# The last stage of a hybrid attention layer in another order: block 2's operands beside block 3's out product, then MLP 2, gates 0 and 2, MLP 3, gate 3

## The chip, the cores and the metric

The kernel runs on one core of one Trainium2 chip. The metric is the device time of one execution in microseconds (us). The kernel before takes 3191.57 us (median of 3 runs, 3189.75 to 3192.46). The core's engines run beside each other: TensorE (PE, matmuls), VectorE (DVE), ScalarE (ACT), GpSimd (POOL) and SyncE (SP, which issues all the transfers named here). [...] Each engine takes its instructions in the order of the program, so an instruction that waits holds up all that stand behind it on its engine; SyncE's transfers are issued in that order too.

## The reference, cut to what matters

One layer with a model width of 1024 over 2048 prompt tokens and 32 sample tokens. Both attentions come first; what follows them, for each token, is:

```python
x = x + concat(attn_a, attn_b) @ w_out              # out product, residual
c = rmsnorm(x, g_mlp)
x = x + relu(c @ w_up) ** 2 @ w_down                # MLP, 1024 -> 4096 -> 1024
x = x + sigmoid(x @ w_ple_gate) * (p @ w_ple_proj)  # gate; p has 256 columns
y = rmsnorm(x, g_final)                             # final rows
```

Everything is float32. Tokens do not meet in these five lines, so blocks of tokens may be done in any order; within a block the lines must follow one another.

## The kernel before, in words

The tokens form four blocks: 0, 1 and 2 of 512, and 3 of 544 with the sample tokens. Activations lie transposed, with the width on the partitions (8 tiles of 128) and the tokens on the free axis. A float32 product is made of three passes: each operand is split into a high part (ScalarE rounds it) and a low part (GpSimd or VectorE subtracts the high one), and `mm3` issues high x high, high x low and low x high (lines 215, 216, 217). Weights are split in the same way, in halves called pieces, as they come in (`wr` is the raw weight; lines 175 and 180 are the splits' instructions on GpSimd and ScalarE, 165 and 186 are those of the GpSimd and VectorE subtraction elsewhere).

`outproj(b)` makes the residual of a block in 8 steps of d: a weight, a load of x (`hd`), 8 x 3 matmuls into `ops`, an addition on VectorE (line 935), the square for the norm, and a store into the scratch tensor `hS` in HBM. `oload(b)` loads the attention's output of a block (`oraw`), normalizes half of it (line 910) and splits it into `oact`. `colnorm(b)` makes from the squares the reciprocal norm `r` (lines 1017 to 1020 on VectorE are its last steps).

Blocks 0 and 1 go through their MLP (`mlp`) with plain products. Blocks 2 and 3 use `mlp7`, in which each up product of a 2 x 2 partition is made of seven products of half the width. Its operands are seven sums of the normalized rows, each split in two, made by `cparts(b)` in four quarters k: two loads of rows from `hS` into `tmp`, two scalings by gain and norm (line 976), five VectorE splits and two GpSimd splits (line 165) and four VectorE sums (lines 988 to 991); ScalarE makes the seven high parts. The results lie in `cs` (14 tiles for one block). In `mlp7`, up products go to `ups`, VectorE forms their combinations (line 1135), ScalarE squares (lines 1139, 1140), and the down products `dps` are added to `h` by VectorE (line 1124). It makes its own sums of the weights on VectorE (lines 1163 to 1166).

`gate(b)` splits the 8 tiles of h into `hu` (or into the tiles of `cs` for block 3), loads the split p (`pT`) and makes, for each of 8 d, a gate product `gps` and a projection `pps`, a sigmoid on ScalarE and VectorE, and an addition to h. `hu` and `pT` together take all 20 tiles of the ring `u` in the pool `uh`. `final(b)` transposes h by TensorE (`yp`), takes the squares (`junk`), scales and stores y.

`weave(main, side, step)` runs two generators in turn: after every step-th yield of `main` one step of `side`, and the rest of `side` at the end. The order of the program on each engine follows from the order of these calls. All loads and stores of this part are issued by SyncE (line 156). Tiles come from pools with rings; a new tile waits for the last reader of the one whose place it takes. Pools on the left are a stack, so that what is opened after another was closed lies on its place.

The last stage, in `run`, starts when MLP 1 and gate 1 are done:

1. out product 2, with the loads of block 3's attention output (`oload(3)`, into the pool `acth`);
2. out product 3; behind its first step the norm `r2`; behind its end `acth` is closed and `cs` opened on its place. The pool `hh`, with two buffers for h, lies elsewhere and has been open from the start, so that h of block 0 can be loaded early;
3. gate 0, with the norm `r3` behind its first step and `cparts(2)` beside it;
4. MLP 2, with `final(0)` beside it; h of block 2 is loaded ahead of it;
5. gate 2, with `cparts(3)` beside it;
6. MLP 3, with `final(2)` beside it; h of block 3 is loaded ahead of it;
7. gate 3 and `final(3)` together.

Of the kernel before, what the change touches and what calls it, by code (L numbers as in the profile page):

```python
# [12 lines left out]
F32 = mybir.dt.float32  # L13
# [6 lines left out]
P = 128  # L20
D = 1024
# [12 lines left out]
BLK = 544  # L34
# [48 lines left out]
def drain(gen):  # L83
    for _ in gen:
        pass
# [57 lines left out]
class Kern:  # L143
# [1115 lines left out]
                        self.pool_tt(hv, hv, sg, ALU.add)  # L1259
                yield  # L1260

    def final(self, b, h, up, fk, mm, md=None):
        nc, a = self.nc, self.a
        t0 = 512 * b
        sts, yns = {}, {}
        phased = md is not None

        def side(c0, tn, q):
            if phased:
                sts[c0] = st_all[:, c0 // P]  # L1270
            elif q == 0:
                sts[c0] = fk.tile([P, 2], F32, tag="fst", bufs=6, name="fst")
            st = sts[c0]
            yp = (md if phased and q == 1 else mm).tile([P, 512], F32, tag="mm", name="yp")
            for k in range(4):
                nc.tensor.transpose(yp[:tn, P * k : P * k + P], h[:, 4 * q + k, c0 : c0 + tn], self.ident)
            if phased and q == 1:
                yns[c0, q] = yp
            else:
                yns[c0, q] = up.tile([P, BLK], F32, tag="u", name="yn")[:, :512]  # L1280
                if phased:
                    nc.vector.tensor_tensor(yns[c0, q][:tn], yp[:tn], self.gf[:tn, :512], op=ALU.mult)
                else:
                    nc.vector.tensor_copy(yns[c0, q][:tn], yp[:tn])
            junk = up.tile([P, BLK], F32, tag="u", name="junk")[:tn, :512]
            nc.scalar.activation(junk, yp[:tn], AF.Square, accum_out=st[:tn, q : q + 1])

        if phased:
            st_all = fk.tile([P, 5, 2], F32, tag="fsa", name="fsa")
            nc.gpsimd.memset(st_all, 1.0)  # L1290
            for c0, tn in toks(b):
                side(c0, tn, 0)
                yield
        def emit(c0, tn, r):
            tt = t0 + c0
            dst = a["y_prompt"][0, tt : tt + tn] if tt < SP else a["y_sample"][0, tt - SP : tt - SP + tn]
            for q in range(2):
                src = yn = yns[c0, q]
                if phased and q == 1:
                    yn = up.tile([P, BLK], F32, tag="u", name="yo")[:, :512]  # L1300
                g = self.gf[:tn, 512 * q : 512 * q + 512]
                if phased and q == 0:
                    nc.scalar.activation(yn[:tn], src[:tn], AF.Copy, scale=r)
                else:
                    nc.vector.scalar_tensor_tensor(yn[:tn], src[:tn], r, g, op0=ALU.mult, op1=ALU.mult)
                self.dma(dst[:, 512 * q : 512 * q + 512], yn[:tn])

        if phased:
            for c0, tn in toks(b):
                side(c0, tn, 1)  # L1310
            ss = fk.tile([P, 5], F32, tag="fss", name="fss")
            nc.vector.tensor_tensor(ss, st_all[:, :, 0], st_all[:, :, 1], op=ALU.add)
            r = self.rsqrt(fk, ss, 5, 1.0 / D, EPS, nc.vector, "rfa")
            for i, (c0, tn) in enumerate(toks(b)):
                emit(c0, tn, r[:tn, i : i + 1])
            return
        for c0, tn in toks(b):
            side(c0, tn, 0)
            side(c0, tn, 1)
            st = sts[c0]  # L1320
            nc.vector.tensor_tensor(st[:tn, 0:1], st[:tn, 0:1], st[:tn, 1:2], op=ALU.add)
            emit(c0, tn, self.rsqrt(fk, st[:tn, 0:1], 1, 1.0 / D, EPS, nc.vector, "rf", tn, 5))
            yield

    def run(self):
        tc, nc, a = self.tc, self.nc, self.a
        with ExitStack() as top:
# [13 lines left out]
            mm = opened(top, "mm", MM, PSUM)  # L1341
# [94 lines left out]
            wk = opened(sq_, "wk", 1)  # L1436
# [49 lines left out]
            self.nt = 8  # L1486
            self.rawp = Rings((self.wp, "wr"), (wk, "wr"))
            self.gfin(fk)
            hh = opened(top, "hh", 2, side="right")
            with ExitStack() as x:  # L1490
                act = Sized(opened(x, "acth", 2), BLK, True)
                weave(self.outproj(2, wk, oa[2], md, acc[2]), self.oload(3, wk, act, oa), 1, 0, OW)
                g = self.outproj(3, wk, oa[3], md, acc[3])
                next(g)
                r2 = self.colnorm(acc[2][0], 2, 1.0 / D, wk, mm, "mm", None)
                drain(g)
            cs = Sized(opened(top, "cs", 14), None)
            ops = {}
            h = hload(hh, BLK, 0)
            g = self.gate(0, h, up, None, md, wk)  # L1500
            next(g)
            r3 = self.colnorm(acc[3][0], 3, 1.0 / D, wk, mm, "mm", None)
            weave(g, self.cparts(2, wk, cs, ops, r2), 1)
            f = self.final(0, h, up, fk, mm)
            h = hload(hh, BLK, 2)
            m = self.mlp7(2, h, ops[2], wk, up, mm, md)
            for _ in range(2):
                next(m)
            weave(m, f, 1)
            g = self.gate(2, h, up, None, md, wk)  # L1510
            next(g)
            weave(g, self.cparts(3, wk, cs, ops, r3), 1)
            f = self.final(2, h, up, fk, mm)
            h = hload(hh, BLK, 3)
            m = self.mlp7(3, h, ops[3], wk, up, mm, md)
            for _ in range(2):
# [53 lines left out]
```

## Time and profile before

| what | value |
|---|---|
| median of the runs | 3191.57 us (3189.75 to 3192.46, 3 runs) |
| the profiled execution's own time | 3197.78 us |
| its span, first to last instruction | 3196.0 us |
| mean granted clock of TensorE in it | 0.977 of full speed |
| out product 3 | 2213.7 to 2272.4 us of the span |
| gate 0 | 2272.4 to 2329.0 us |
| MLP 2 | 2329.0 to 2671 us |
| gate 2 | 2671 to 2743 us |
| MLP 3 | 2743 to 3117 us |
| gate 3 and the last final rows | 3117 to 3196 us |

The stages are cut where TensorE's instructions change; at a boundary a few matmuls of one stage stand among those of the next. The profile gives for each engine the busy time, and for each group of instructions (line, engine, operation, output and input tiles) the number, the mean duration and the idle time just ahead of them with what ended it. A row of the waits has the engine and line that waited, what ended the wait, the total, the number and the longest. A row of the timeline has the start, the duration, the engine and line, the operation and its tiles, and in square brackets the idle time ahead of it with its releaser. A row of the transfers has the number, the size and the median time from issue to landing. Matmuls overlap, so that the distance between two starts, and not the duration, is the pace. [...]

### The profile page before, as it was taken

To read this page: it belongs to the slowest core of one execution; us is meant where nothing else is said; L and a number is where in the kernel's file an instruction comes from. 1 tells how busy PE (TensorE), PEld (TensorE's weight loads), DVE (VectorE), ACT (ScalarE), POOL (GpSimd) and SP (SyncE) were. 2 spreads that over 40 slices of the span, in tenths; PEclk is the share of its full clock that TensorE was granted. 3 is DMA by queue.
4 is the path that set the end of the run, shared out by engine and by line. 5 is a ranking of instruction groups with operands and counts; after the bars stand their busy time and mean duration, and the time that the engine had idled before them with its cause. 6 is when DMAs were issued, how large, how long until landed. Compare 5 with 4: busy or idle time off the path is not lost.

```text
span 3196.0 us, 53414 instructions
## 1 busy us (share of the span) xinstructions
PE 3037.6 (95%) x18265; PEld 2694.5 (84%) x18265; DVE 1851.6 (58%) x4448; ACT 1885.5 (59%) x4166; POOL 1887.4 (59%) x2572
## 2 busy tenths in 40 slices
PE   8998989999999998999999999998999999899998
PEld 7787877899987787877788888877888888899998
DVE  5157774544454554666765666435577665776663
ACT  5256775766665764676665666554555555554445
POOL 4466546333335544565554555677787778867674
PEclk9998999999999999999999999999999999999999
DMA  8787767977688745555554534446524334233331
GB/s 267 237 242 224 208 191 237 251 227 206 199 244 227 209 130 134 149 165 138 170 158 139 148 111 119 126 147 216 182 86 147 106 99 127 93 100 108 92 114 55
DMA packets 512505, 521.61 MB, mean 163 GB/s; under 512 B 37949, under 2 KB 393601, under 8 KB 512233
## 3 DMA queue, kind: packets, MB, share of 16 engines
q1 hardware_dynamic: 512232, 518.19, 55.2%
q8 instruction: 145, 2.38, 0.3%
q14 instruction: 128, 1.04, 0.1%
HBM read 412.08 MB, written 109.95 MB: 163 GB/s over the span
## 4 chain that ended last, share of the span: by engine, by line
PE 68%; DMA 12%; DVE 10%; ACT 4%; issue 3%; POOL 2%; SPq 1%; DVEq 0%; ACTq 0%; POOLq 0%
PE dps L215 6%; PE dps L216 6%; PE dps L217 6%; PE ups L215 6%; PE ups L216 6%; PE ups L217 6%; PE s L632 3%; PE qps L215 3%; PE qps L216 3%; PE qps L217 3%; DMA oraw<-oT 2%; PE ob L842 2%; PE tpb L817 1%; PE tpp L704 1%; DMA wr<-w_up 1%
## 5 line engine op out<-in xcount | busy, mean ns | idle before, releaser
L175 POOL TENSOR_TENSOR wl<-wr,wh 128x256 fp32r<-128x256 f32 x648 | 474.5, 764 | 333.6 <-ACT wh L180 328.0
L180 ACT ACTIVATE piece<-wr 128x512 fp32r<-128x512 f32 x412 | 252.9, 626 | 289.0 <-PE ups L216 144.0
L175 POOL TENSOR_TENSOR piece<-wr,piece 128x256 fp32r<-128x256 f32 x416 | 336.4, 834 | 103.2 <-ACT piece L180 87.8
L180 ACT ACTIVATE wh<-wr 128x1024 fp32r<-128x1024 f32 x228 | 240.8, 1057 | 198.5 <-PE qps L216 51.7
L165 POOL TENSOR_TENSOR wl<-wr,wh 128x256 fp32r<-128x256 f32 x264 | 197.9, 781 | 185.8 <-ACT wh L180 180.4
L215 PE MATMUL ups<-cs,piece 128*128 128x256 f32 (+1 forms) x896 | 257.3, 288 | 7.8 <-ACT piece L180 6.1
L217 PE MATMUL ups<-cs,piece 128*128 128x256 f32 (+1 forms) x896 | 257.4, 287 | 5.6 <-POOL piece L175 5.6
L216 PE MATMUL ups<-cs,piece 128*128 128x256 f32 (+1 forms) x896 | 256.6, 286 | 0.5 <-DVE cs L186 0.5
L216 PE MATMUL dps<-ul,piece 128*128 128x272 f32 (+1 forms) x768 | 247.7, 324 | 1.3 <-DVE ul L186 1.3
L217 PE MATMUL dps<-uh,piece 128*128 128x272 f32 (+1 forms) x768 | 247.5, 324 | 1.2 <-POOL piece L165 1.2
L215 PE MATMUL dps<-uh,piece 128*128 128x272 f32 (+1 forms) x768 | 246.2, 324 | 1.0 <-DVE h L1124 0.8
L165 POOL TENSOR_TENSOR piece<-wr,piece 128x256 fp32r<-128x256 f32 x280 | 223.5, 829 | 25.1 <-ACT piece L180 24.3
L1124 DVE TENSOR_TENSOR h<-h,dps 128x272 f32<-128x272 f32 (+1 forms) x384 | 190.8, 515 | 81.5 <-PE dps L217 80.5
L215 PE MATMUL qps<-aH,wh 128*128 128x512 f32 (+1 forms) x640 | 230.8, 361 | 5.8 <-DVE ql L475 4.3
L215 PE MATMUL dps<-uh,wh 128*128 128x512 f32 x512 | 209.5, 409 | 20.8 <-ACT wh L180 7.2
L216 PE MATMUL qps<-aL,wh 128*128 128x512 f32 (+1 forms) x640 | 229.2, 358 | 0.0
L217 PE MATMUL qps<-aH,wl 128*128 128x512 f32 (+1 forms) x640 | 228.4, 357 | 0.0
L1083 DVE TENSOR_TENSOR h<-h,dps 128x512 f32<-128x512 f32 x256 | 174.2, 682 | 82.3 <-PE dps L217 77.6
L632 PE MATMUL s<-ka,q 128*128 128x512 f32 (+3 forms) x768 | 188.6, 349 | 19.4 <-DMA ka<-kS 10.0
L215 PE MATMUL ups<-cH,wh 128*128 128x512 f32 x512 | 202.7, 396 | 0.5 <-DVE h L1083 0.4
L216 PE MATMUL dps<-ul,wh 128*128 128x512 f32 x512 | 202.1, 395 | 0.0
L217 PE MATMUL dps<-uh,wl 128*128 128x512 f32 x512 | 202.1, 395 | 0.0
(298 smaller groups left out, 9764.7 us busy)
## 6 DMA issues: line engine op xcount, KB each, us to landing
wr<-w_up SPq DMA_DIRECT2D x128, 512.0 KB, 4.1
wr<-w_down SPq DMA_DIRECT2D x128, 512.0 KB, 3.7
wr<-w_in SPq DMA_DIRECT2D x74, 512.0 KB, 4.6
q<-qS SPq DMA_DIRECT2D x128, 256.0 KB, 5.2
v<-vSa SPq DMA_DIRECT2D x64, 512.0 KB, 3.9
ka<-kS SPq DMA_DIRECT2D x32, 512.0 KB, 7.8
wr<-w_out SPq DMA_DIRECT2D x32, 512.0 KB, 5.0
wr<-w_ple_gate SPq DMA_DIRECT2D x32, 512.0 KB, 4.1
```

The source lines that it names most:

```text
L165: nc.gpsimd.tensor_tensor(out[:, sl], a[:, sl], b[:, sl], op=op)
L175: nc.gpsimd.tensor_tensor(out[:, sl], a[:, sl], b[:, sl], op=op)
L180: nc.scalar.activation(hi, raw, AF.Copy)
L215: nc.tensor.matmul(ps, lh, rh, start=start and i == 0, stop=False)
L216: nc.tensor.matmul(ps, lh, rl, start=False, stop=False)
L217: nc.tensor.matmul(ps, ll, rh, start=False, stop=stop and i == n - 1)
L632: nc.tensor.matmul(s, q[:, m, hl, P * qi : P * qi + nr], kt[:, m, k0 - kb : k0 - kb + n], start=hl == 0, stop=hl == 1)
L704: nc.tensor.transpose(tp[:kn, x, :nr], w[:nr, P * i : P * i + kn], self.ident[:nr, :nr])
L817: nc.tensor.transpose(tp[:kn, x, :nr], e[:, P * (x0 + x) : P * (x0 + x) + kn], self.ident[:nr, :nr])
L842: nc.tensor.matmul(o[:, qa:qb], vt, pt[:kn, i - kfirst, qa:qb], start=x == 0 and y == 0, stop=x == len(order) - 1 and y == 1,)
L1083: nc.vector.tensor_tensor(hv, hv, ps, op=ALU.add)
L1124: nc.vector.tensor_tensor(hv, hv, ps, op=ALU.add)
```

## The change

The steps of the last stage are put in another order, and two pools change place:

- `cs` is opened at the start of the stage, on the right; `hh` is opened behind `acth`, on its place. So h of the first block can only be loaded when out product 3's last matmul has read `acth`.
- `cparts(2)` runs beside out product 3, with one quarter for every two of its steps, on the norm that was `r2`.
- h of block 2 and then h of block 0 are loaded, and MLP 2 comes right behind out product 3. Block 3's norm stands behind its first step. Nothing runs beside it.
- gate 0 follows, with `cparts(3)` beside it.
- gate 2 follows gate 0, with `final(0)` beside it. Its tiles `yn` and `junk` come from the ring `tmp` of `wk` (8 buffers) and not from `u`, which both gates use.
- MLP 3 and gate 3 are as before.

```diff
-    def final(self, b, h, up, fk, mm, md=None):
+    def final(self, b, h, up, fk, mm, md=None, wk=None):
...
+        def row(name):
+            if wk is not None:
+                return wk.tile([P, BLK], F32, tag="tmp", bufs=self.nt, name=name)
+            return up.tile([P, BLK], F32, tag="u", name=name)
...
-                yns[c0, q] = up.tile([P, BLK], F32, tag="u", name="yn")[:, :512]
+                yns[c0, q] = row("yn")[:, :512]
...
-            junk = up.tile([P, BLK], F32, tag="u", name="junk")[:tn, :512]
+            junk = row("junk")[:tn, :512]
...
-            hh = opened(top, "hh", 2, side="right")
+            cs = Sized(opened(top, "cs", 14, side="right"), None)
+            ops = {}
             with ExitStack() as x:
                 act = Sized(opened(x, "acth", 2), BLK, True)
                 weave(self.outproj(2, wk, oa[2], md, acc[2]), self.oload(3, wk, act, oa), 1, 0, OW)
                 g = self.outproj(3, wk, oa[3], md, acc[3])
                 next(g)
-                r2 = self.colnorm(acc[2][0], 2, 1.0 / D, wk, mm, "mm", None)
-                drain(g)
-            cs = Sized(opened(top, "cs", 14), None)
-            ops = {}
+                r = self.colnorm(acc[2][0], 2, 1.0 / D, wk, mm, "mm", None)
+                weave(g, self.cparts(2, wk, cs, ops, r), 2)
+            hh = opened(top, "hh", 2)
+            h2 = hload(hh, BLK, 2)
             h = hload(hh, BLK, 0)
+            m = self.mlp7(2, h2, ops[2], wk, up, mm, md)
+            next(m)
+            r = self.colnorm(acc[3][0], 3, 1.0 / D, wk, mm, "mm", None)
+            drain(m)
             g = self.gate(0, h, up, None, md, wk)
             next(g)
-            r3 = self.colnorm(acc[3][0], 3, 1.0 / D, wk, mm, "mm", None)
-            weave(g, self.cparts(2, wk, cs, ops, r2), 1)
-            f = self.final(0, h, up, fk, mm)
-            h = hload(hh, BLK, 2)
-            m = self.mlp7(2, h, ops[2], wk, up, mm, md)
-            for _ in range(2):
-                next(m)
-            weave(m, f, 1)
-            g = self.gate(2, h, up, None, md, wk)
+            weave(g, self.cparts(3, wk, cs, ops, r), 1)
+            g = self.gate(2, h2, up, None, md, wk)
             next(g)
-            weave(g, self.cparts(3, wk, cs, ops, r3), 1)
-            f = self.final(2, h, up, fk, mm)
+            weave(g, self.final(0, h, up, fk, mm, wk=wk), 1)
+            f = self.final(2, h2, up, fk, mm)
             h = hload(hh, BLK, 3)
             m = self.mlp7(3, h, ops[3], wk, up, mm, md)
```

## The prediction

> **What bounds the kernel now.** First the page: busy time by engine, and the chain that ended last.
>
> ```profile
> PE 3037.6 (95%) x18265; PEld 2694.5 (84%) x18265; DVE 1851.6 (58%) x4448; ACT 1885.5 (59%) x4166; POOL 1887.4 (59%) x2572
> ...
> PE 68%; DMA 12%; DVE 10%; ACT 4%; issue 3%; POOL 2%; SPq 1%; DVEq 0%; ACTq 0%; POOLq 0%
> ```
>
> TensorE is busy for 95% of the span and carries 68% of the chain. The change issues the same matmuls in another order, so only what TensorE loses can move: idle time, and time at a lower granted clock. So I cut the last stage into its parts by windows (length; busy time and instructions of PE, PEld, DVE, ACT, POOL; clock; DMA share; GB/s).
>
> ```profile
> 2213.70:2272.40 58.70, 52.59 (x385) 51.89 (x384) 20.89 (x31) 23.80 (x41) 48.91 (x62) 0.91 0.80 245
> 2272.40:2329.00 56.60, 56.60 (x248) 45.87 (x247) 46.08 (x66) 33.59 (x72) 45.66 (x51) 1.00 0.35 112
> 2329.00:2351.60 22.60, 16.98 (x124) 16.30 (x122) 15.13 (x26) 15.83 (x32) 20.14 (x23) 0.85 0.21 71
> 2351.60:2671.00 319.40, 316.94 (x1973) 282.92 (x1974) 213.64 (x344) 168.24 (x315) 248.23 (x305) 1.00 0.37 115
> 2671.00:2743.00 72.00, 71.64 (x324) 58.29 (x322) 53.60 (x75) 41.48 (x84) 59.16 (x68) 1.00 0.38 120
> 2743.00:2770.00 27.00, 19.34 (x127) 18.48 (x127) 16.44 (x23) 16.04 (x31) 23.41 (x29) 0.81 0.33 98
> 2770.00:3117.00 347.00, 345.32 (x2752) 344.83 (x2751) 237.11 (x478) 173.32 (x315) 246.30 (x310) 1.00 0.33 103
> ```
>
> In order: out product 3, gate 0, start of MLP 2, rest of MLP 2, gate 2, start of MLP 3, rest of MLP 3. Both gates and the steady MLPs leave TensorE almost no idle time at clock 1.00. Three windows lose: the out product (6.1 us idle, clock 0.91), the start of MLP 2 (5.6, 0.85), the start of MLP 3 (7.7, 0.81). What ended that idle time, from the waits of TensorE (total, times, longest):
>
> ```profile
> PE ups L215 <- ACT piece L180: 6.1, 2, 3.6
> PE ops L215 <- ACT oact L180: 6.1, 2, 4.1
> PE ups L217 <- POOL piece L175: 5.6, 2, 2.9
> ...
> PE dps L217 <- POOL piece L165: 1.2, 2, 1.0
> ```
>
> The starts of the MLPs wait for weight pieces split on ScalarE and GpSimd, which stand there behind the work on the MLP's operands; the out product waits for its own activations; the dps row is of small waits in MLP 2.
>
> To price each loss I need the full-clock pace. In MLP 2 the matmuls run in a row:
>
> ```profile
> 2346.08 0.28 PE L216 MATMUL ups<-cs,piece 128*128 128x256 f32 x1
> ...
> 2351.19 0.28 PE L217 MATMUL ups<-cs,piece 128*128 128x256 f32 x1
> 2351.66 0.49 PE L215 MATMUL dps<-uh,piece 128*128 128x512 f32 x1 [0.20 <-ACT uh L180]
> ```
>
> From 2346.08 to 2351.19 there are 43 steps: 5.11/43 = 0.119 us for one of 256 columns; for 272 columns the last window gives 345.32/2752 = 0.1255. So:
> - out product 3: 58.7 - 385 x 0.1255 = 10.4 us lost.
> - start of MLP 2, up to its first down product (dps) at 2351.66: 22.6 - 124 x 0.119 = 7.8.
> - start of MLP 3: 27.0 - 127 x 0.1255 = 11.1.
>
> Each is more than the idle time, since the clock is lower after it:
>
> ```profile
> 2234.00:2236.30 2.30, 0.32 (x3) 0.10 (x1) 0.92 (x1) 0.68 (x2) 2.30 (x4) 1.00 0.45 123
> 2236.30:2241.30 5.00, 4.97 (x24) 4.71 (x25) 3.50 (x6) 2.96 (x6) 2.57 (x4) 0.66 1.02 378
> ```
>
> A gap of 2.0 us is followed by 5 us at a mean clock of 0.66, that is (1 - 0.66) x 5 = 1.7 us of work lost on top.
>
> **The change part by part.**
>
> *(1) Out product 3 (gain).* The 2 MB loads of h no longer run beside it. Block 0's is issued here (SyncE's queue), and the two take 9.3 us to land (median):
>
> ```profile
> 2207.75 0.57 SPq L156 DMA_DIRECT2D h<-hS  x1
> ...
> 2214.57 0.44 SPq L156 DMA_DIRECT2D oraw<-oT  x1
> ```
>
> ```profile
> h<-hS SPq DMA_DIRECT2D x2, 2048.0 KB, 9.3
> ```
>
> The oraw load of 2214.57 stands behind it; in a later turn VectorE waits for oraw 5.1 us:
>
> ```profile
> 2234.67 0.92 DVE L910 SCALAR_TENSOR_TENSOR oraw<-oraw,g_b_s,rb 128x544 f32<-128x544 f32 x1 [5.10 <-DMA oraw<-oT]
> ...
> 2246.94 1.22 DVE L1020 TENSOR_TENSOR r<-r,sqacc 128x512 f32<-128x512 f32 x1
> ```
>
> Each turn of that loop is load, VectorE, store, next load, so the delay adds up. I estimate oraw 4.5, 6 and 7.5 us earlier in the three turns, out product 3 ending 4 us earlier (2268 for 2272.4; bounds 0 and 10.4), and the last line, which ends block 2's norm r at 2248.2, at about 2237: 7.5 from oraw, 4 from TensorE's product for the norm, which no longer follows two gaps (bounds 2237 and 2248).
>
> *(2) Block 2's operands beside out product 3, and MLP 2 right behind it (loss).* This is the largest term. In before the operands were made beside gate 0, which gives 56.6 us of cover; now they have from 2237 to 2268, and MLP 2 needs them at once. Their VectorE work, in before beside gate 0:
>
> ```profile
> L186 DVE TENSOR_TENSOR cs<-tmp,cs 128x256 fp32r<-128x256 f32 x20 | 13.7, 706 | 0.1
> L976 DVE SCALAR_TENSOR_TENSOR tmp<-tmp,g_mlp_s,r 128x512 f32<-128x512 f32 x8 | 7.4, 920 | 0.0
> ...
> L989 DVE TENSOR_TENSOR tmp<-tmp 128x256 f32<-128x256 f32 x4 | 3.0, 742 | 0.1
> L990 DVE TENSOR_TENSOR tmp<-tmp 128x256 f32<-128x256 f32 x4 | 2.9, 730 | 0.2
> L988 DVE TENSOR_TENSOR tmp<-tmp 128x256 f32<-128x256 f32 x4 | 2.6, 659 | 0.0
> L991 DVE TENSOR_TENSOR tmp<-tmp 128x256 f32<-128x256 f32 x4 | 2.5, 630 | 0.1
> ```
>
> One quarter (k) has two L976, five cs splits, and L988 to L991: 2 x 0.92 + 5 x 0.706 + 2.76 = 8.1 us. Beside it VectorE adds each product to the residual and prepares MLP 2's first weights, which I take as 3 and 5 us, so 11 us for the first quarter and 13 for the second. The tmp loads of quarters 1, 2 and 3 stand on SyncE's queue behind stores of block 3's hS, each waiting for an addition that VectorE does only after the quarter before; each turn adds a load:
>
> ```profile
> tmp<-hS SPq DMA_DIRECT2D x8, 272.0 KB, 4.2
> ```
>
> In a burst those took 4.2; for two issued alone I take 3 to 3.5. So quarter 0 is done at 2237 + 11 = 2248, quarter 1 starts at 2251 and ends at 2264, quarter 2's rows land at 2267.5. After VectorE's first 4 us on it (2271.5) SyncE is past the store of d = 6 and issues **h of block 2, h of block 0**, since their pool lies where block 3's activations were and the program puts them here. The first lands after 9.3 us; the second follows at the 378 GB/s of the window at 2236.30, 2.1 MB / 378 = 5.5, taken as 6: 2287. Quarter 3's two tmp loads, issued at 2279 after the last store, land behind both, as oraw did behind h at 2214.57: 2289. The first split of it reaches TensorE at 2291, the last operand at about 2301 (8.1 us and three weight steps).
>
> TensorE meanwhile: out product ends 2268; three quarters of seven products, 63 x 0.119 = 7.5, held by quarter 2 until about 2277, done at 2282; idle to 2291; 40 matmuls at half clock, 8.5, up to the last operand at 2301; 32 more to 2305; then the sums, the squaring and the split (ACT), as in before:
>
> ```profile
> 2348.75 0.63 ACT L1139 ACTIVATE r<-r 128x512 f32<-128x512 f32 x1 [2.39 <-DVE r L1135]
> ```
>
> From the first Relu there to the first dps at 2351.66 are 2.9 us; with the VectorE sums ahead of it (4.5) the first dps comes at 2308.5.
>
> From the start of out product 3 that is 2308.5 - 2213.7 = 94.8, against 58.7 + 22.6 = 81.3: **+13.5**. Block 3's norm products (about 10 x 0.1255) are in it and leave gate 0: **-1**. Clock after the last gap, like the row above: **+2**. Bounds of the three together: the operands in time, 48.3 + 125 x 0.119 = 63.2, or -18; r not earlier (all 11 later), +25. Nearest row: the walk's, so I take +14.5.
>
> [...]
>
> *(3) Start of MLP 3 (gain).* Block 3's operands are made beside gate 0, a whole gate ahead. In before their rows came late in gate 2:
>
> ```profile
> DVE tmp L976 <- DMA tmp<-hS: 12.4, 1, 12.4
> ```
>
> Now block 3's r is there when gate 0 starts and VectorE no longer has them while MLP 3's weights are split. Of its waits (above) the first down product's stays:
>
> ```profile
> L216 PE MATMUL dps<-ul,piece 128*128 128x272 f32 x5 | 1.5, 310 | 0.9 <-DVE ul L186 0.9
> ```
>
> The waits for pieces go with their clock; the 0.9 (ul) stays, and half as much of its kind: 11.1 - 1.4 = **-9.7** (bounds 0 and -11.1).
>
> *(4) Block 0's final rows in gate 2, not in MLP 2.* The window of MLP 2 has 319.4 - 316.9 = 2.5 us idle; about 2 are those rows' (the dps wait for POOL above, 1.2, and smaller ones): **-2**. Beside gate 2 they meet no additions of MLP sums; **+0.5** (0 to 2).
>
> *(5) Gate 2 right behind gate 0 (loss).* Both take hu and pT from the same 20 buffers, so gate 2's splits of h wait for gate 0's last matmuls. In before gate 2 made them under MLP 2's end:
>
> ```profile
> L165 POOL TENSOR_TENSOR hu<-h,hu 128x256 fp32r<-128x256 f32 x8 | 6.7, 861 | 1.9 <-ACT hu L180 1.9
> ```
>
> GpSimd's half is 6.7 us. If none is covered: 6.7 + 1.7 for the clock = 8.4; if TensorE's last products of gate 0 cover it, 0. ScalarE and VectorE make the first ones in about 1.5 us, so I take one gap as in the row at 2234 less its cover: **+3**.
>
> Sum: 14.5 - 9.7 - 2 + 0.5 + 3 = **+6.3 us**. The profiled execution is 3197.78 (span 3196.0 and 1.78 around it): 3204.1. The median, 3191.57, is 6.2 lower; the same sum gives **3198**.
>
> [...]
>
> **The rivals.**
> - *A, the forecast*, +6.3, with +1 to +12 as its own range. For it: the SP rows and the four quarters' order. Against: it needs each of four turns to be as long as walked.
> - *B, gate 2 stalls fully.* (5) at 8.4, and one more half-clock stretch (1.7) in MLP 2's start: 14.5 - 9.7 - 2 + 0.5 + 10 = +13: 3205. For it: POOL is busy 45.7 of 56.6 us beside gate 0. It decides over A when GpSimd ends the splits over 5 us behind gate 0's last matmul.
> - *C, quarter 3 isn't held up by the h loads* (not slower). If its rows land with VectorE done with quarter 2 (2279), the first dps comes at 2297: (2) falls by 11.5 and its clock term: +6.3 - 11.5 - 2 = -7: 3184; with r's chain faster too, down to -18. From rows landing before about 2283 on, the sum is not above zero. Against it: one queue, in order, as at 2214.57.
> - *D, nothing changes*: TensorE's order is other, but losses move as they are: 0, within 4: 3191.6. For it: 95% busy. The equal-loss case needs (2) to cost what (3) and (4) give, 11.
>
> **How the numbers follow.** A 0.43, B 0.20, C 0.27, D 0.10. A comparison of this kernel can tell about 0.2%, 6.4 us, from no change. A gives 0.28 slower and 0.15 within; B 0.20 slower; C 0.20 faster and 0.07 within; D 0.10 within. So faster 0.20, same 0.32, slower 0.48. Range: from 3182, which holds C's -7 and a little more, to 3209, which holds B and (2) at r's late bound (25 - 9.7 - 2 + 0.5 + 3 = +17); left out are C's long end (about 0.10) and B with that bound together.
>
> **What would show it.** (1) no 5.1 us wait for oraw, out product 3 in some 54 us. (2) TensorE idle 8 to 10 us on cs from ACT, some 15 us behind the out product's end, and tmp landing right behind the second h; the first dps some 95 us after out product 3 begins. (3) no gap over 1 us at the start of MLP 3. (4) MLP 2's steady part without dps waits. (5) a gap of 1 to 3 us on hu at gate 2. Wrong would be: tmp landing ahead of h (C), or a gap over 5 us at gate 2 (B).

## The result, and the profile after

| | before | after |
|---|---|---|
| median, run beside each other | 3192.46 us (7 runs, 3189.75 to 3202.43) | 3210.28 us (7 runs, 3199.31 to 3217.89) |
| profiled execution | 3197.78 us | 3205.29 us |
| its span | 3196.0 us | 3203.5 us |
| mean granted clock | 0.977 | 0.976 |

The ratio after to before is 1.0042, with a 95% interval of 1.0022 to 1.0061: some 13 us slower (7 to 19.5). The two medians lie 17.8 us apart, within that interval. A second comparison (`a0_after`, below) gave 1.0042 again, with 1.0029 to 1.0056.

The two spans differ by less, 7.5 us, and that has its own reason. Out product 2, ahead of which the two programs are alike, starts at 2164.68 us in before's profile and at 2160.59 in after's; over all profiles of this study it starts between 2152.7 and 2168.6. So the times of two profiles are compared from that start on. From there to the end of the span before takes 1031.3 us and after 1042.9: **+11.6**. The second profile of after gives 1043.2. That is the number to explain.

The page of after: busy time by engine, and the chain that ended last.

```profile
PE 3042.3 (95%) x18265; PEld 2698.8 (84%) x18265; DVE 1854.4 (58%) x4448; ACT 1886.2 (59%) x4166; POOL 1872.3 (58%) x2572
...
PE 70%; DMA 12%; DVE 9%; ACT 4%; issue 2%; POOL 1%; SPq 1%; DVEq 0%; ACTq 0%; POOLq 0%
```

The same 18265 matmuls, the same 95%. Nothing on this level tells the two kernels apart; the stages do. After's windows, with the columns as in the prediction: out product 3, start of MLP 2, rest of MLP 2, both gates, start of MLP 3, rest of MLP 3, and then three short stretches that are used further down.

```profile
2209.50:2264.70 55.20, 51.25 (x387) 50.29 (x386) 36.51 (x54) 23.10 (x46) 41.11 (x50) 0.97 0.60 185
2264.70:2308.00 43.30, 24.81 (x138) 22.26 (x136) 31.07 (x51) 20.68 (x46) 26.52 (x30) 0.80 0.56 204
2308.00:2630.90 322.90, 322.84 (x1980) 288.62 (x1981) 206.60 (x315) 165.99 (x292) 245.12 (x310) 0.99 0.34 102
2630.90:2752.90 122.00, 118.05 (x513) 95.29 (x513) 83.52 (x123) 76.02 (x163) 97.87 (x119) 0.97 0.45 141
2752.90:2780.00 27.10, 24.87 (x179) 24.01 (x178) 14.92 (x23) 16.02 (x31) 25.14 (x31) 0.94 0.32 100
2780.00:3124.80 344.80, 343.15 (x2736) 342.68 (x2735) 234.52 (x474) 173.02 (x315) 243.50 (x307) 1.00 0.33 103
2279.40:2287.00 7.60, 0.10 (x2) 0.05 (x1) 1.30 (x2) 0.42 (x1) 0.02 (x1) 0.81 0.96 371
2690.30:2697.20 6.90, 6.04 (x14) 4.78 (x15) 3.10 (x4) 6.90 (x14) 6.77 (x10) 0.51 0.00 0
2772.20:2775.70 3.50, 3.42 (x15) 3.42 (x16) 1.77 (x4) 1.96 (x4) 3.50 (x5) 0.51 0.39 121
```

The second row is the loss: of 43.3 us TensorE is idle 18.5, at a clock of 0.80. In before the start of MLP 2 took 22.6. Cut by the first matmul of each stage (in before gate 2 then begins at 2682.2 and MLP 3 at 2738.7, not at 2671 and 2743 as in the table of the stages), the account is:

| part | before | after | difference |
|---|---|---|---|
| start of out product 3 to the first down product (gate 0 taken out in before) | 81.7 | 98.6 | +16.9 |
| of it out product 3 | 59.0 | 55.2 | -3.8 |
| MLP 2 from its first down product | 330.6 | 322.9 | -7.7 |
| gates 0 and 2 | 112.7 | 121.9 | +9.2 |
| MLP 3 | 378.6 | 371.9 | -6.7 |
| out product 2, gate 3 and the last rows | 127.7 | 127.6 | -0.1 |
| sum | | | +11.6 |

The 32 transposes of block 0's final rows moved from MLP 2 into the gates; in before they stand in four runs of 8 at 0.099 us each, so 3.2 us of the rows of MLP 2 and of the gates are the same work in another place. The waits of TensorE in after, from out product 3 to the start of MLP 3 (total, times, longest):

```profile
PE ups L215 <- ACT cs L180: 10.6, 3, 7.5
PE dps L215 <- ACT uh L180: 4.1, 2, 3.0
PE gps L215 <- ACT hu L180: 4.0, 1, 4.0
PE ops L215 <- ACT oact L180: 3.6, 2, 3.1
PE ups L216 <- DVE cs L186: 2.7, 3, 2.1
```

The three waits for pieces in before's list (12.9 us) are down to 0.2. In their place stand block 2's operands (cs), the split of the squares (uh) and gate 2's split of h (hu).

Where the operands were late is read on VectorE, in the scalings that begin a quarter; "[6.31 <-DMA tmp<-hS]" says that VectorE stood idle for 6.31 us until the rows had landed:

```profile
2234.33 1.26 DVE L1020 TENSOR_TENSOR r<-r,sqacc 128x512 f32<-128x512 f32 x1
...
2250.80 1.66 DVE L976 SCALAR_TENSOR_TENSOR tmp<-tmp,g_mlp_s,r 128x512 f32<-128x512 f32 x2 [3.18 <-DMA tmp<-hS]
...
2264.81 1.59 DVE L976 SCALAR_TENSOR_TENSOR tmp<-tmp,g_mlp_s,r 128x512 f32<-128x512 f32 x2 [2.94 <-DMA tmp<-hS]
...
2285.70 1.41 DVE L976 SCALAR_TENSOR_TENSOR tmp<-tmp,g_mlp_s,r 128x512 f32<-128x512 f32 x2 [6.31 <-DMA tmp<-hS]
```

The norm is done at 2235.6, and quarters 1, 2 and 3 begin at 2250.8, 2264.8 and 2285.7. SyncE's queue shows why the last one is further off than the others:

```profile
2268.26 0.32 SPq L156 DMA_DIRECT2D hS<-hd  x1
2268.62 0.42 SPq L156 DMA_DIRECT2D hd<-xT  x1
2269.10 1.57 SPq L156 DMA_DIRECT2D h<-hS  x2
2275.14 0.33 SPq L156 DMA_DIRECT2D hS<-hd  x1
2275.51 1.89 SPq L156 DMA_DIRECT2D tmp<-hS  x2
```

```profile
h<-hS SPq DMA_DIRECT2D x2, 2048.0 KB, 10.0
...
tmp<-hS SPq DMA_DIRECT2D x2, 256.0 KB, 10.2
```

The two loads of h go out at 2269; the rows of quarter 3, issued at 2275.5 behind the store of 2275.14, take 10.2 us (those of quarters 1 and 2 took 3.2 and 3.5). While they land the window at 2279.40 (above) has TensorE busy for 0.10 of 7.60 us and the transfers at 371 GB/s. Then the matmuls that had waited run, the squares are split, and the first down product starts 98.6 us behind out product 3's start:

```profile
2308.06 0.79 PE L215 MATMUL dps<-uh,piece 128*128 128x512 f32 x1 [2.97 <-ACT uh L180]
...
2691.16 0.79 PE L215 MATMUL gps<-hu,piece 128*128 128x512 f32 x1 [3.95 <-ACT hu L180]
...
2770.76 0.52 PE L215 MATMUL dps<-uh,piece 128*128 128x272 f32 x2 [1.12 <-ACT uh L180]
```

The other two rows are the gap at gate 2 and the one that is left at the start of MLP 3.

### The profile page after: what moved, and what is told of

It reads as the page before. It is cut to its first block, busy times and chain, and to the rows that moved or that the text cites. A ratio compares the mean times of both kernels' runs of the same rounds, so it can differ in the third digit from the quotient of the medians.

```text
span 3203.5 us, 53420 instructions
## 1 busy us (share of the span) xinstructions
PE 3042.3 (95%) x18265; PEld 2698.8 (84%) x18265; DVE 1854.4 (58%) x4448; ACT 1886.2 (59%) x4166; POOL 1872.3 (58%) x2572
## 4 chain that ended last, share of the span: by engine, by line
PE 70%; DMA 12%; DVE 9%; ACT 4%; issue 2%; POOL 1%; SPq 1%; DVEq 0%; ACTq 0%; POOLq 0%
PE dps L215 7%; PE dps L216 7%; PE dps L217 6%; PE ups L215 6%; PE ups L216 6%; PE ups L217 6%; PE s L632 3%; PE qps L215 3%; PE qps L217 3%; PE qps L216 3%; DMA oraw<-oT 2%; PE ob L842 2%; PE tpb L817 2%; PE gps L215 2%; DMA tmp<-hS 2%
## 5 line engine op out<-in xcount | busy, mean ns | idle before, releaser
L216 PE MATMUL ups<-cL,wh 128*128 128x512 f32 x512 | 201.8, 394 | 0.2 <-DVE stb L809 0.2
```

The source lines that it names most:

```text
L216: nc.tensor.matmul(ps, lh, rl, start=False, stop=False)
```

## The experiments

The theory after the comparison: the loss is MLP 2 standing right behind out product 3 with operands that come late, and it has two parts. **H**: the two 2 MB loads of h stand ahead of quarter 3's rows. **T**: the turns. One quarter is woven into every second step of the out product, and each quarter's rows stand on SyncE's queue behind a store that waits for an addition made only after the quarter before. The three kernels behind the repeat (`a0_after`) tell H from T. The ratios are to before on the same chip, with 95% intervals.

**After once more** (`a0_after`), as the base of this group.

> The changed kernel once more, as the base on this chip. Theory (the queue: MLP 2's last quarter of operands lands behind both loads of h, and TensorE waits for it): ratio 1.002 to 1.006, TensorE idle about 7.5 us on cs in front of the last quarter, first down product of MLP 2 some 98 us behind the start of out product 3, a gap of 4 us at gate 2. Rival (noise of the clock: the measured 0.4% is chance): ratio within 0.9985 to 1.0015 here.

Measured: 1.0042 (1.0029 to 1.0056); 3209.65 against 3196.43 us. The first down product comes 99.9 us behind out product 3's start, and VectorE's waits for rows are 13.9 in four, the longest 6.6 (after: 12.9, 6.3). The picture repeats.

**The loads of h later** (`e1_h0_behind`).

```diff
-            h2 = hload(hh, BLK, 2)
-            h = hload(hh, BLK, 0)
+            h2 = hh.tile([P, 8, BLK], F32, tag="h", name="h")
             m = self.mlp7(2, h2, ops[2], wk, up, mm, md)
             next(m)
+            self.dma(h2[:, :, : BN[2]], self.hS[:, :, 512 * 2 : 512 * 2 + BN[2]])
             r = self.colnorm(acc[3][0], 3, 1.0 / D, wk, mm, "mm", None)
+            for _ in range(4):
+                next(m)
+            h = hload(hh, BLK, 0)
             drain(m)
```

> The changed kernel with the load of block 0's h issued behind the last quarter's rows; block 2's h stays ahead of them. Theory (the queue): the last quarter's rows land one load of h, 5 to 6 us, earlier, VectorE's wait for them falls from 6.3 us to about 1, the first down product comes 5 us earlier; time 4 to 7 us below the changed kernel. Rival (VectorE: the four quarters, one behind the other, set the time, whatever lies in the queue): VectorE still ends the last quarter where it did, 0 to 1 us.

Measured: 1.0025 (1.0013 to 1.0038), 5.4 us less than `a0_after` by the ratios (0.0017 of 3196). On SyncE h of block 2 still went ahead of the last rows (2278.9 and 2285.5), h of block 0 behind them. VectorE's waits for rows, and TensorE's for cs, in it:

```profile
DVE tmp L976 <- DMA tmp<-hS: 9.8, 4, 3.3
```

```profile
PE ups L215 <- ACT cs L180: 6.8, 2, 4.2
```

The longest wait for rows falls from 6.6 to 3.3, as long as the other quarters', and the first down product comes at 95.9 instead of 99.9. The rows take 6.5 us to land instead of 10.2. So H is there and is worth some 4 us by the first down product, 5 by the ratio (whose interval overlaps that of `a0_after`). Waits of about 3 us for every quarter but the first stay.

**Both loads of h behind the last rows** (`e4_h_last`): as above, and ahead of h2's load a copy of one column that hangs on the first operand of quarter 3, so that the load can't be issued earlier.

```diff
+            nc.vector.tensor_copy(h2[:, 0, :1], ops[2]["b11"][0][:, 3, :1].bitcast(F32))
             self.dma(h2[:, :, : BN[2]], self.hS[:, :, 512 * 2 : 512 * 2 + BN[2]])
```

> The changed kernel with both loads of h held back until the last quarter's first part is made (one tiny copy on VectorE into h makes them wait; the loads then overwrite it). Theory (the queue): rows land as early as VectorE can take them (idle of 6.3 us gone), first down product 6 to 8 us earlier, time 6 to 9 us below the changed kernel, if h itself is still there for the first down sums (it would land at about 23 us behind the out product's end plus 15). Rival (VectorE): 0 to 1 us. A third: h comes too late for the down sums, and a wait on h takes the place of the one removed: as slow as before or slower.

Measured: 1.0029 (1.0018 to 1.0041), 4.2 us less than `a0_after`; not to be told from `e1_h0_behind`. On SyncE the last rows now go out at 2282.8, the loads of h at 2283.8 and 2290.2. The waits:

```profile
DVE tmp L976 <- DMA tmp<-hS: 10.1, 4, 3.2
```

```profile
PE ups L215 <- ACT cs L180: 5.1, 3, 2.6
...
PE dps L215 <- ACT uh L180: 4.5, 1, 4.5
```

With neither load of h ahead of them the rows are waited for as long as in `e1_h0_behind`, and the first down product comes at 95.4. The rows take 5.1 us to land. The gain is less than the 6 to 9 us expected: H is 4 to 5 us, of a loss of 17. The rest must lie elsewhere.

**One quarter for every step** (`e2_quarters`); the loads of h stay where after has them.

```diff
-                weave(g, self.cparts(2, wk, cs, ops, r), 2)
+                weave(g, self.cparts(2, wk, cs, ops, r), 1)
```

> The changed kernel with one quarter of block 2's operands for every step of out product 3 instead of every second. All row loads then stand ahead of the loads of h and no quarter waits for a store behind the quarter before. Theory (the queue, and the turns over the stores): VectorE's waits for rows between the quarters (3.2, 2.9 and 6.3 us in the changed kernel, 12.4 in all) go, the operands are there about 12 us earlier, the first down product 10 to 13 us earlier, and with the half clock behind the gaps the time is 11 to 17 us below the changed kernel, about level with or below the kernel before. Rival (VectorE): VectorE was busy with the quarters anyway, and the additions of out product 3 now come late behind them: out product 3 stalls for its banks, gain below 4 us.

Measured: **0.9984** (0.9976 to 0.9993), 18.5 us less than `a0_after` by the ratios. The waits for rows are all but gone, and one wait of TensorE for cs remains:

```profile
DVE tmp L976 <- DMA tmp<-hS: 0.4, 1, 0.4
```

```profile
PE ups L215 <- ACT cs L180: 3.2, 1, 3.2
```

The rows are issued at 2234.7, 2242.1, 2251.0 and 2260.7, the loads of h only from 2282.5 on:

```profile
2241.75 0.32 SPq L156 DMA_DIRECT2D hS<-hd  x1
2242.12 0.91 SPq L156 DMA_DIRECT2D tmp<-hS  x2
...
2282.50 0.57 SPq L156 DMA_DIRECT2D h<-hS  x1
```

The turns are still there, since each quarter's rows stand behind a store. But the addition of the very next step comes early on VectorE (at 2240.95, ahead of quarter 0's splits), where in after the addition of the step behind that one came at their end (2246.67), so the rows now land while VectorE is still at work on the quarter before. It is not an earlier start that helps: quarter 0 begins 26.4 us behind out product 3's start here and 26.5 in after (28.0 in `e4_h_last`), but quarter 3 at 52.6 instead of 76.2 (72.5). The first down product comes 82.5 us behind out product 3's start, where after has 98.6 and before, with gate 0 taken out, 81.7. T is the larger part, some 13 of the 17 us by subtraction of H, and H bites only because T brings quarter 3 so late. What holds this kernel now is VectorE itself, as its window from 2240 on shows (third busy figure, 27.49 of 27.70):

```profile
2240.00:2267.70 27.70, 27.70 (x223) 27.70 (x222) 27.49 (x41) 12.76 (x30) 21.13 (x23) 1.00 0.54 170
```

**The same once more** (`e5_e2_again`, on another chip).

> The kernel with one quarter of block 2's operands per step of out product 3, once more, as the base on this chip. Theory (the turns over the stores cost most of the change's loss): ratio 0.9975 to 0.9995 again. Rival (chance): 1.000 to 1.004.

Measured: 0.999 (0.9979 to 1.0002); the first down product at 82.7. With `e12_base` (below, 0.9989, 0.9975 to 1.0002) there are three comparisons of this kernel: 0.1% to 0.16% below before, of which the first alone is clear of no change.

Two questions were left: what the gap of 4 us at gate 2 is, and where before's loss at the start of MLP 3 came from.

**The first quarter of block 3's operands earlier, in before** (`e6_early3`), to undo the wait of 12.4 us for rows to which the prediction tied that loss.

```diff
+            c = self.cparts(3, wk, cs, ops, r3)
+            next(c)
             g = self.gate(2, h, up, None, md, wk)
             next(g)
-            weave(g, self.cparts(3, wk, cs, ops, r3), 1)
+            weave(g, c, 1)
```

> The kernel before, its order kept, with the first quarter of block 3's operands begun ahead of gate 2 instead of beside its second product. Theory (what the change gains at the start of MLP 3 is only that block 3's operands are no longer late): VectorE's wait of 12.4 us for rows in gate 2 goes, the gaps of 3.6 and 2.7 us at the start of MLP 3 go or shrink by half, 5 to 10 us faster than the kernel before (ratio 0.997 to 0.9985), without the change's order. Rival (MLP 3's weights are late because GpSimd and ScalarE are full in gate 2, whatever comes early): the gaps stay, within 2 us.

Measured: 0.9991 (0.9978 to 1.0004), not to be told from before. The wait for rows stayed, now for the next quarter's, and TensorE has one wait for a piece in gate 2 and one at the start of MLP 3.

```profile
DVE tmp L976 <- DMA tmp<-hS: 13.7, 1, 13.7
```

```profile
PE gps L217 <- POOL piece L175: 3.0, 1, 3.0
...
PE ups L217 <- POOL piece L175: 3.0, 1, 3.0
```

The work had moved, and most of the loss with it: by the profiles MLP 3 takes 374.2 us instead of 378.6, and gate 2 59.7 instead of 56.4. Where the wait of 12.4 us comes from is read on SyncE in before:

```profile
2681.17 12.24 SPq L156 DMA_DIRECT2D wr<-w_ple_gate  x3
2693.50 1.01 SPq L156 DMA_DIRECT2D tmp<-hS  x2
```

The rows stand on the queue behind three loads of gate weights, and each of these waited for GpSimd's split of a piece (9.6 us in three waits from 2680 to 2694), which frees the raw weights' tile. In `e6_early3` the next quarter's rows stand behind three such loads again (2675.9 to 2686.5). So the rows were late because GpSimd's splits were, and one quarter earlier did not change that.

**Gate 0 on other tiles** (`e7_gate0_cs`). By the prediction's term (5), gate 2 waits since both gates take `hu` from the same ring. Here gate 0 takes the tiles of `cs`, as gate 3 does, so block 3's operands move beside gate 2 and block 0's final rows behind it.

```diff
-            g = self.gate(0, h, up, None, md, wk)
-            next(g)
-            weave(g, self.cparts(3, wk, cs, ops, r), 1)
+            drain(self.gate(0, h, up, cs, md))
             g = self.gate(2, h2, up, None, md, wk)
             next(g)
-            weave(g, self.final(0, h, up, fk, mm, wk=wk), 1)
+            weave(g, self.cparts(3, wk, cs, ops, r), 1)
+            drain(self.final(0, h, up, fk, mm, wk=wk))
```

> The changed kernel with gate 0's splits of h in the tiles of cs, so that gate 2's splits find their own buffers free, and with block 3's operands beside gate 2 as in the kernel before (cs is taken during gate 0); block 0's final rows come behind gate 2. Two terms of the prediction are thus exchanged: the gap at gate 2 (3.9 us idle and 1.7 of clock) should go, and the loss at the start of MLP 3 (11 us in the kernel before, about 3 in the changed one) should come back. Theory: no gap over 1 us at gate 2, gaps of 5 us or more at the start of MLP 3, 3 to 8 us slower than the changed kernel (ratio 1.005 to 1.007). Rival (the gap at gate 2 comes from the backlog of sigmoids on ScalarE and not from the shared buffers): it stays at 3 to 4 us, and the time is 8 to 13 us above the changed kernel.

Measured: 1.0118 (1.0096 to 1.014), some 24 us above `a0_after` by the ratios (on another chip), more than either forecast. TensorE's waits from MLP 2's end to the start of MLP 3:

```profile
PE dps L216 <- DVE ul L186: 7.1, 1, 7.1
PE ups L215 <- ACT t L1133: 6.3, 1, 6.3
PE yp L1281 <- ACT junk L1291: 5.0, 4, 3.2
...
PE gps L215 <- ACT hu L180: 1.0, 1, 1.0
```

The gap at gate 2 falls from 4.0 to 1.0 us, but the block 3 operands left gate 0 in the same edit, so this doesn't tell the ring from what was woven in. The other rows are the price of the edit, as it seems: gate 0's splits with nothing between them ahead of MLP 2's last down products, and the final rows alone on TensorE.

The next kernels leave the tiles as they are. From 2685.4 on ScalarE is at work in after almost without a break, with gate 0's sigmoids (lines 1235 to 1240), and the first split of hu (line 180) comes right behind them:

```profile
2686.27 0.61 ACT L1240 ACTIVATE sig<-sig 128x512 f32<-128x512 f32 x1
...
2689.96 0.63 ACT L1240 ACTIVATE sig<-sig 128x512 f32<-128x512 f32 x1 [0.76 <-DVE sig L1239]
2690.50 0.61 ACT L180 ACTIVATE hu<-h 128x512 fp32r<-128x512 f32 x1
```

The last tile of `hu` had been free for 5 us by then, since gate 0's last gate product ended at 2685.5. So the new theory is a backlog: the seven splits of each woven quarter, and ScalarE's waits for the VectorE results that they split (1.5, 0.9, 0.8 and 0.3 us from 2677 to 2685.4), push gate 0's sigmoids back, and gate 2's first split stands behind them. The sigmoids of gate 0's first three products begin 0.4 to 0.7 us behind the end of their product, those of its last four 7.2 to 9.0 us. If so, taking some of the quarters out of gate 0, with the ring as it is, must close the gap.

**Two quarters, or one, of block 3's operands ahead of gate 0** (`e8_early2`, `e10_early1`), both with `e2_quarters`' edit as well. The diff of the second; the first has `next(c)` twice.

```diff
             drain(m)
+            c = self.cparts(3, wk, cs, ops, r)
+            next(c)
             g = self.gate(0, h, up, None, md, wk)
             next(g)
-            weave(g, self.cparts(3, wk, cs, ops, r), 1)
+            weave(g, c, 1)
```

> The base of this call with two of the four quarters of block 3's operands begun at the end of MLP 2, ahead of gate 0, so that ScalarE and VectorE are through with them before gate 0 ends. Theory (the gap at gate 2 is ScalarE's backlog: the sigmoids of gate 0's last products wait behind the splits of the quarters, and h's splits behind them): the gap falls from 3.9 us to below 2, with the clock 2 to 5 us faster than the base. Rival (shared buffers: h's splits wait for gate 0's last matmuls, nothing else): the gap stays at 3.5 to 4 us, no gain; and if the quarters disturb MLP 2's last sums, 1 to 3 us slower.

Measured: 0.9985 (0.9972 to 0.9999), no gain that can be told from the base (0.999). TensorE's waits around gate 0 and gate 2 have no hu; the largest is a new one, at MLP 2's end:

```profile
PE dps L215 <- DVE h L1124: 3.4, 1, 3.4
```

The gap at gate 2 is gone without a change of the ring, which is the backlog's prediction, and so is the backlog: the sigmoids of gate 0's last three products begin 0.3 to 0.4 us behind their product. It was paid for elsewhere: two quarters on VectorE ahead of MLP 2's last additions.

> The same base with one of the four quarters of block 3's operands begun ahead of gate 0 (two took the gap at gate 2 away and brought one of 3.4 us at the end of MLP 2). Theory: the gap at gate 2 falls to below 2 us and the one at the end of MLP 2 stays below 1, 2 to 5 us faster than the base (ratio 0.9972 to 0.9985). Rival (both are one backlog that only changes place): the sum of the two gaps stays at 3.5 us, within 1.5 us of the base.

Measured: **0.9971** (0.9959 to 0.9982), 3187.70 against 3197.32 us. The last four sigmoids come 7.0 to 3.6 us behind their product, and from 2600 to 2700 TensorE waits for nothing but p:

```profile
PE pps L216 <- DMA pT<-pS: 0.3, 1, 0.3
PE pps L215 <- DMA pT<-pS: 0.2, 1, 0.2
```

**`e2_quarters` as their base on this chip** (`e12_base`).

> The base of this call, the kernel with one quarter per step of out product 3, for the comparison on one chip. From its two calls so far (0.9984 and 0.9990): 0.998 to 0.9995.

Measured: 0.9989 (0.9975 to 1.0002), 3195.02 us. In the same stretch:

```profile
PE gps L215 <- ACT hu L180: 3.9, 1, 3.9
```

Both gates take 120.75 us here and 116.25 in `e10_early1`, 4.5 less: the gap, and the half clock behind it. In this pair of profiles MLP 3 gives 2.3 of that back (372.9 us for 370.6), and the intervals of the two ratios overlap a little, so what the last step is worth is not settled. Against before and after the result is clear: the order with one quarter beside every step and one quarter ahead of gate 0 beats both, 0.3% below before.

**One more split on GpSimd** (`e9_t3_pool`; `e11_both` with `e10_early1`'s edit too). As VectorE holds `e2_quarters`, the low part of t3 goes to GpSimd for block 2.

```diff
-            parts(("t2", "dve"), ("t1", "dve"), ("t3", "dve"), ("t4", "pool"))
+            parts(("t2", "dve"), ("t1", "dve"), ("t3", "pool" if b == 2 else "dve"), ("t4", "pool"))
```

> The kernel with one quarter per step of out product 3, and one of VectorE's five splits of each quarter of block 2 given to GpSimd. Theory (once the turns over the stores are gone, VectorE is the bound: it is busy 27.49 of 27.70 us in the second half of out product 3): four splits of 0.4 to 0.95 us less on it, the last operands 2 to 4 us earlier, first down product as much earlier, 1 to 4 us faster than without (ratio 0.9975 to 0.9985). Rival (GpSimd, busy 21 of 27.7 us there, becomes the bound with 1.4 us more per quarter): the weights' pieces come later, no gain or 1 to 5 us slower.

Measured: 0.9998 (0.9989 to 1.0006), 2.9 us more than `e12_base` by the ratios, with intervals that overlap. The first down product comes at 84.4 instead of 81.8, and TensorE has a wait for GpSimd's split:

```profile
PE ups L216 <- POOL cs L165: 2.0, 1, 2.0
```

> Both edits together, as the best version that the runs point to. If both theories hold: 3 to 8 us faster than the base, ratio 0.996 to 0.998; if both rivals hold, the base or some us above it.

Measured: 0.9983 (0.9974 to 0.9992), likewise no better than `e10_early1` alone (0.9971). There was no gain, as the rival had it. That GpSimd, which splits the weights, has no more room there than VectorE fits its new wait, but was not tested further.

## Why the prediction was right, and which terms were mis-sized

The forecast was +6.3 us and a median of 3198; the profiles gave +11.6, the ratio some +13 (3191.57 x 1.0042 is 3205). The number alone doesn't choose between the likeliest case (A, +1 to +12) and rival B (+13). The traces do: B's sign, a gap over 5 us at gate 2, did not come (3.95), and the largest term of A, quarters that come in turns with the last one behind both loads of h, was found in place. Two other terms had their cause wrong, and one sum came out by luck. By its steps:

**(1) Out product 3: the size as forecast, the way there only in part.** It takes 55.2 us instead of 59.0 (-3.8; forecast -4). But VectorE still waits for oraw: 3.2, 4.0 and 0.2 us in its three turns, where before has 0.4, 0.5 and 5.1. Counted from out product 3's start the three scalings come 4.2, 3.4 and 5.3 us earlier, not 4.5, 6 and 7.5, and the norm 8.4 earlier, not 11. Of before's three loads of oraw only that of 2214.57 went out while a load of h was under way. The one that VectorE waited 5.1 us for was issued at 2228.68, when the first h had landed (at 2217.8) and the second was not yet issued (2233.98), so this wait was not made by a load of h ahead of it.

**(2) MLP 2's start: right in kind, 3.4 us short.** Walked against seen: quarters 1, 2 and 3 begin at 2251, 2267.5 and 2289 against 2250.8, 2264.8 and 2285.7; the first down product at 2308.5 against 2308.06. The walk fits in absolute times, but it was counted from out product 3's start, which in after is 4.2 us earlier (2209.5), so that after has 98.6 where the walk has 94.8 (3.8 more; 0.4 of them are in before's side, 81.7 for 81.3). Two of its steps took longer than walked: the norm came 26.1 us behind that start (2235.6 - 2209.5) instead of 23.3, and from quarter 3's rows to the first down product it was 22.4 us (2308.1 - 2285.7) instead of 19.5. Those two are 5.7; 1.9 came back in the quarters between. The norm's 2.8 go back to (1).

On the cause the walk had both parts, but its rival C, and the point from which C was to decide, hung on h alone. `e4_h_last` has C's condition (no load of h ahead of the rows) and gains 4.2 us where C had 13.3 between it and the forecast. Without h the rows still landed only 72.5 us behind out product 3's start, where C took 65.3 (2279 - 2213.7). `e2_quarters` shows what was worth that much: the turns, at 13 of the 17 us. The sign of the forecast held because it had walked the four turns one by one.

Quarter 3's rows took 10.2 us from issue to landing behind both loads of h (4 MB, after), 6.5 behind one load of 2 MB (`e1_h0_behind`) and 5.1 behind none (`e4_h_last`). In after they landed 16.6 us after the first load of h was issued (2285.7 - 2269.1; the walk had 17.5), and VectorE waited 6.3 us for them.

**(3) MLP 3's start: gain of 6.7 instead of 9.7.** The waits for pieces that led there went, as said. No run shows by itself that the earlier place of block 3's operands did it: `e6_early3` moved one quarter and took away half of those waits, and `e7_gate0_cs` changed too much else. But two small gaps of 1.12 us (uh) and 0.48 (ul) stayed, and with them a stretch of 3.4 us at half clock (window at 2772.20: 0.51). After's start loses 27.1 - 179 x 0.1255 = 4.6 us, where the prediction left 1.4. In `a0_after` the same two gaps (1.13 and 0.50) brought no half clock. Its window of the same stretch, with the clock at 1.00, is:

```profile
2753.00:2780.00 27.00, 24.58 (x188) 23.56 (x187) 15.07 (x23) 15.87 (x31) 25.58 (x31) 1.00 0.35 102
```

That is a loss of 27.0 - 188 x 0.1255 = 3.4, and MLP 3 takes 370.7 us there, a gain of some 8. So about 1 of the missing 3 is the clock, which may come or not; the other 2 are gaps and small waits that the term took as gone.

**(4) and (5) The rest of MLP 2 and the gates: right in sum by luck, wrong one by one.** From the first down product to the end of the gates the change is -7.7 + 9.2 = +1.5; the forecast's terms there (-1, +2, -2, +0.5, +3) give +2.5. Within it the gates are dearer than (5): the 9.2 hold the 3.2 of moved transposes, the gap of 3.95 and some 2.7 of the 6.0 us at half clock behind it (window at 2690.30: 0.51; the first 0.8 of the 6.83 us lie in the gap; matmuls of 512 columns start 0.427 us apart there, and 0.232 apart from 2697.49 on). Block 3's norm, which (2) counted at about 10 matmuls and -1, is 4 matmuls and -0.2. MLP 2 is cheaper than (4): of its -7.7, -3.2 are the transposes, some -1 the up products that now stand ahead of the first down product (44 of 448 of each pass instead of 41, 9 x 0.119), +1.5 a stretch of 3.4 at half clock (from 2308.06; matmuls of 256 columns start 0.214 us apart there, and 0.119 at full clock), and -3.7 the waits ahead of its down products, which (4) put at -2: from start to start, the 767 steps that end in a down product take 171.8 us in before and 168.1 in after. No wait of its own is left in its steady part, as forecast. What makes up the last -1.2 was not taken apart. By these paces matmuls start 1.8 times as far apart at half clock, and the 1.7 us that the prediction put on such a stretch is an estimated 1.5.

Term (5) had the place of the gap right, its size too small (1 to 3 forecast, 3.95 seen, and the half clock behind it) and its cause wrong. The ring `u` was not what gate 2 waited for: `e8_early2` and `e10_early1` leave the ring alone and the gap goes when quarters leave gate 0. It was ScalarE's order behind the woven splits. Rival B, a gap over 5 us by GpSimd, did not come.

So the sum missed 5.3 us: 3.4 in (2), 3.0 in (3), -1.0 in (4) and (5), and -0.1 outside all of them.

## What to carry to other kernels

When side work is woven into a stage, price its turns: a load that is issued behind a store, which waits for an addition, which waits for the side work of the turn before, makes one round trip per turn (quarter 3's rows went out at 2275.51, right behind the store of 2275.14), and here these turns cost some 13 us, the 4 MB of transfers in their way 4 to 5. A stage that has just lost its cover wants its operands made as early as the stage ahead allows; `e2_quarters` did this with one figure and turned +0.42% into about -0.1%. And when a wait for a tile appears, look at what the engine that writes it did just before: a backlog of woven work looks like a shared buffer until that work is moved.

## What the runs showed of the hardware

- Short gaps of TensorE of the same length were not followed by the same clock. At MLP 3's start in after, gaps of 1.12 and 0.48 us were followed by 3.4 us at a clock of 0.51; in `a0_after` gaps of 1.13 and 0.50 at the same place by none. Of the 11 profiles with a gap of 1.1 us at this place, with 0.3 to 0.5 close behind, 6 show the half clock behind it (after, `e1_h0_behind`, `e5_e2_again`, `e9_t3_pool`, `e10_early1`, `e12_base`) and 5 don't. In `e6_early3` the gap of 3.0 us in gate 2 was followed by none, and that of 3.0 us at MLP 3's start by 3.4 us at half clock.
- After almost the same gap at gate 2 the half clock lasted either 3.4 or 6.8 us: 3.41 behind gaps of 3.89 (`a0_after`), 3.92 (`e2_quarters`), 3.94 (`e12_base`) and 4.00 (`e4_h_last`), 6.83 behind 3.73 (`e5_e2_again`), 3.75 (`e1_h0_behind`), 3.95 (after) and 4.18 (`e9_t3_pool`).
- Code that is the same in both kernels, all ahead of out product 2, ended anywhere from 2152.7 to 2168.6 us over the profiles. One pair of spans can't show a change of 10 us; the distance from a common point can.
